# A written order for GpSimd in attention, and a few operations moved in the opening of a transformer layer

## The chip, the cores and the metric

The kernel runs on one core of a Trainium2 chip. Its time is the device time of one execution in microseconds (us). The engines are named as in the profile: PE is TensorE (matrix products), PEld its weight load, DVE is VectorE, ACT is ScalarE, POOL is GpSimd, SP is SyncE, which only issues DMA transfers. Each engine works through its own queue of instructions in the order in which the program lists them.

## The reference

One layer over 1024 latent tokens and 256 context tokens, model width 1024, all in float32. Cut to what matters here:

```
m_lat = silu(c) @ w_mod + b_mod            # six modulation vectors; m_ctx the same from c_ctx
h_lat = rms_norm(x, norm1_g) * (1 + sc1) + sh1
h_ctx = rms_norm(ctx, norm1_g) * (1 + csc1) + csh1
rq, rk, rv, rg, dq, dk, dv = split(h @ w_in)          # rotary positions on q and k
ret = sum over 2 directions of group_norm(retention(rq, rk, rv, decay))    # chunks of 128, states carried
y_ret = silu(rg) * ret
p   = softmax over keys, for two score maps per head  # 4 heads, 1280 keys, queries in blocks of 128
a   = p[0] - lam * p[1]
y_diff = rms_norm(a @ dv) * subln_g * 0.8             # per head, over its 128 columns
x   = x + g1 * (concat(y_ret, y_diff) @ w_out)
h2  = rms_norm(x, norm2_g) * (1 + sc2) + sh2
u   = conv3(h2 @ w_up);  x = x + g2 * ((silu(u_a) * u_b) @ w_down)
out = rms_norm(x, final_g)
```

## The kernel before

**Precision.** A float32 matrix is split in two parts, hi (a cast by ACT) and lo (the difference, by DVE or POOL). A product is three matmuls, hi by hi, hi by lo, lo by hi (`passes`, lines 133 to 135).

**Stages.** The program runs through one core's queues in this order:

- the *opening*: the modulation vectors of the first norm, the norm of the tokens, and the first projection (block 6 of w_in, the values of attention). Per block of 128 model columns `modulate` (lines 585 to 600) transposes four row-scaled token tiles on PE (L590), lets ACT write hi (L593), DVE a float32 copy `tmp` (L598), and DVE or POOL the lo part (L600). `scale` (L584) multiplies a token tile by its row's factor, `power` makes that factor (L115), `mod_part` (L562) makes the modulation and `mod_row` (L566) and `mod_sums` (L573, L574) bring it in place, `w_split` (L621, L623) splits the weights. Token tiles 0 to 3 form half 0, tiles 4 to 7 half 1.
- the other *projections* (blocks 5, 2, 1, 3, 0, 4). Each takes its weights by `split_slice` (lines 193 to 199): load on SP, cast on ACT (L198), difference on DVE (L199).
- *retention*, as side work beside the last projections. `beside(generator, rate, due)` sets a generator, and `tick`, called for each k-step of a projection (three matmuls), adds `rate` to a counter that starts at `due`; for each whole unit of the counter one step of the generator puts out its instructions. Retention's generator is `outputs` (lines 369 to 406), with rate 1.35. Its products of states start at L269; the states are summed on DVE (L466).
- *attention*: 32 units, four heads by eight query tiles. Per unit: scores (L940), their least value (L943, DVE), exp (L947, ACT), the ratio of the two sums (L951 and L952, DVE, 128x1), the combined probabilities (L955, DVE, 128x1280), their transposes (L960 on PE, copies L966 on ACT), values (L972 on PE), copy and square (L976, L981 on ACT), e (L983, POOL, 128x1), the sum for the norm (L986, DVE), the power (L987, POOL, 128x1), the scaling (L990, ACT), a transpose (L994, PE), hi (L998, ACT) and lo (L1001, DVE). The table `TAU` gives each of these a time in units; the operations are written in that order, step n after step n, and `in_order` fixes it for the engines of `FORCE`: PE, DVE, ACT and SP, not for POOL.
- beside attention POOL and ACT prepare the output projection, a Strassen-Winograd product of half matrices. `first_tokens` and `out_weights` load 512 columns into `woraw` (five buffers), ACT casts them (L1123 and L1106), POOL subtracts (L1124, L1108). `joined_tokens` (L1128 to 1132) has POOL add hi and lo of the attention result to a float32 tile, a `woraw` too, and issues DMA transfers that add it to sums in DRAM. Other DMA transfers of POOL (L1156 and around) add weights in DRAM. Queries, keys and values of later units are loaded by POOL's queue (L1018, L1021, L1043). `issue_after` holds such a piece back in the scheduler until a power of an earlier unit has been placed.
- the *output projection* and the *MLP*, which the change does not touch.

The order in the opening is the order of the source from `begin` to `in_order(begin)`; what stands outside (such as the first split of the next block, L198 and L199) is placed by the scheduler.

Of the kernel before, what the change touches and what calls it, by code (L numbers as in the profile page):

```python
# [8 lines left out]
F32 = mybir.dt.float32  # L9
F32R = mybir.dt.float32r  # L10
# [59 lines left out]
def r32(ap):  # L70
    return ap.bitcast(F32)
# [3 lines left out]
def kernel(  # L75
# [85 lines left out]
    with ExitStack() as p1:  # L161
# [385 lines left out]
        with ExitStack() as p0:  # L547
# [151 lines left out]
            for k in range(KD):  # L699
# [8 lines left out]
                if k == 1:  # L708
                    mod_sums(2)
                    latents(0, 2)  # L710
                    for t in (2, 3):
                        scale(xs0[t], 2 + t, 3 * P, D)
                    for q in range(2):
                        mod_part(3, q)
                    mod_row(3)
                if k == 4:
                    square(xs1[2], 8)
                    power(8)
                    scale(xs1[0], 6)
# [15 lines left out]
                if k == 0:  # L735
                    for q in range(2):
                        mod_part(2, q)
                    mod_row(2)
                if 0 < k < KD - 2:
                    mod_sums(k + 2)  # L740
                    latents(0, k + 2)
                    if 0 < k < 5:
                        for q in range(2):
                            mod_part(k + 3, q)
                        mod_row(k + 3)
                if k in (0, 2, 4):
                    w_split()
# [65 lines left out]
        wg = stream_block(5)  # L813
        beside(modulations2(), 37 / 156)
# [96 lines left out]
        beside(outputs(), 1.35, -16.0)  # L911
# [182 lines left out]
    def out_weights(srcs, sl, eng=nc.sync, low=nc.vector, lag=0, after=(), free=0):  # L1094
        raws = []
        srcs = [src[:, k, :] for src in srcs for k in range(4)]
        for k in range(len(srcs) + lag):
            if k < len(srcs):
                raw = wo.tile([P, 512], F32, name="woraw", bufs=5)
                wo_loads.append(eng.dma_start(out=raw, in_=srcs[k]))  # L1100
                raws.append(raw)
            yield
            if k >= lag:
# [3 lines left out]
                part = low.tensor_tensor(out=wlo, in0=raws[k - lag], in1=r32(whi), op=ALU.subtract)  # L1107
# [5 lines left out]
    wo_gen = out_weights((A11, ws_d[0]), wo_first, nc.gpsimd, nc.gpsimd, 2)  # L1113

    def first_tokens():
        raws = []
        for h in range(H + 2):
            if h < H:
                raws.append(wo.tile([P, 512], F32, name="woraw", bufs=5))
                nc.gpsimd.dma_start(out=raws[h], in_=yr_d[:, h, :])  # L1120
            yield
            if h > 1:
                nc.scalar.copy(yT[0][1][:, h - 2, :], raws[h - 2])  # L1123
                nc.gpsimd.tensor_tensor(out=yT[1][1][:, h - 2, :], in0=raws[h - 2], in1=r32(yT[0][1][:, h - 2, :]), op=ALU.subtract)  # L1124

    wo_gen = itertools.chain(first_tokens(), wo_gen)

    def joined_tokens(h, half):  # L1128
        raw = wo.tile([P, 512], F32, name="woraw", bufs=5)
        nc.gpsimd.tensor_tensor(out=raw, in0=r32(yT[0][half][:, H + h, :]), in1=r32(yT[1][half][:, H + h, :]), op=ALU.add)  # L1130
        for to in (t4_d,) if half else (t2_d, t3_d):
            nc.gpsimd.dma_start(out=to[:, h, :], in_=raw, accum_op=ALU.add)

    with ExitStack() as p2:
# [6 lines left out]
        for n in range(n_units + 8):  # L1141
# [3 lines left out]
            if n == 9:  # L1145
                with tc.issue_after(units[n - 5].pool_ins.ins):
                    nc.gpsimd.dma_start(out=g1, in_=row_d[0].rearrange("p c -> (p c)").partition_broadcast(P))
            if n in (6, 9, 15, 17, 21, 28):
                with tc.issue_after(units[n - 5].pool_ins.ins):
                    if n == 6:  # L1150
                        nc.gpsimd.dma_start(out=t1_d[:, H - 1, :], in_=yr_d[:, H - 1, :], accum_op=ALU.add)
                    elif n == 9:
                        nc.gpsimd.dma_start(out=t2_d[:, :, :], in_=t1_d[:, :, :])
                    else:
                        i, j, k = {15: (1, 0, 0), 17: (1, 0, 2), 21: (3, 1, 0), 28: (3, 1, 2)}[n]
                        nc.gpsimd.dma_start(out=ws_d[i][:, k : k + 2, :], in_=ws_d[j][:, k : k + 2, :], accum_op=ALU.add)  # L1156
            if n in (14, 21, 29):
                nc.sync.dma_start(out=t4_d[:, (14, 21, 29).index(n), :], in_=t2_d[:, (14, 21, 29).index(n), :])
            for half, when in ((0, (12, 18, 26, 33)), (1, (16, 24, 31))):
                if n in when:  # L1160
                    with tc.issue_after(units[min(n - 5, n_units - 1)].pool_ins.ins):
                        joined_tokens(when.index(n), half)
            for op, t in order:
# [14 lines left out]
        in_order(start)  # L1178
# [756 lines left out]
```

## Time and profile before

| | us |
|---|---|
| median of 3 runs | 1365.8 (1365.76 to 1365.85) |
| profiled execution | 1365.33, of which span 1363.5 |
| opening | 0 to 65 |
| projections, then with retention beside | 65 to 322, 322 to 460 |
| attention | 460 to 635 |
| output projection, MLP | 635 to 775, 775 to 1363.5 |
| PE busy | 1348.6 of 1363.5 (99%) |
| DVE, ACT, POOL busy | 998.3, 749.6, 341.7 |
| mean granted PE clock of the span | 0.998 |

A row of the timeline reads: start, length, engine, line and operation, output <- inputs, shape and type, how many in a row, and in brackets the idle time of that engine just before and what ended it. The end of a matmul in the profile is modelled, and neighbouring matmuls overlap; so how PE proceeds is read from starts, not from ends. A row with x3 lasts from its first start to its last end.

### The profile page before, as it was taken

How to read it: one execution, taken by the hardware profiler on the slowest of the kernel's cores; microseconds unless marked ns; L12 is line 12 of the kernel's file. 1: busy time of each engine (PE TensorE's matmuls, PEld its weight loads, DVE VectorE, ACT ScalarE, POOL GpSimd, SP SyncE). 2: the span in 40 equal slices, each digit the busy share in tenths (PEclk: the TensorE clock that was granted, in tenths of full speed). 3: DMA queues.
4: the chain of work that ended last, by engine and by line, in shares of the span. 5: the costliest groups of instructions: out<-in, count | busy, mean ns of one | idle time of the engine just before them, and what ended most of it. 6: DMA issues, size and time to landing. Idle time of an engine off the chain costs nothing.

```text
span 1363.5 us, 19850 instructions
## 1 busy us (share of the span) xinstructions
PE 1348.6 (99%) x6978; PEld 1134.9 (83%) x6978; DVE 998.3 (73%) x1514; ACT 749.6 (55%) x1429; POOL 341.7 (25%) x433
## 2 busy tenths in 40 slices
PE   9999999999999999999999999999999999999997
PEld 6788888888898899998887788888888888888886
DVE  4746874425775899897989986677776777798856
ACT  4643312424765789997547555445554455455543
POOL 1210004403776436543021222221222110000001
PEclk9999999999999999999999999999999999999999
DMA  9567897655866769855954898988888875963523
GB/s 369 216 255 241 296 314 245 190 181 157 214 174 168 177 153 182 169 109 157 342 166 113 194 233 217 224 218 226 214 213 214 220 193 172 371 214 101 177 93 124
DMA packets 130492, 279.71 MB, mean 205 GB/s; under 512 B 13700, under 2 KB 34948, under 8 KB 129480
## 3 DMA queue, kind: packets, MB, share of 16 engines
q1 hardware_dynamic: 100440, 212.99, 45.8%
q0 software_dynamic: 29376, 64.00, 25.6%
q10 hardware_dynamic: 576, 1.44, 0.3%
q8 instruction: 55, 0.90, 0.3%
q14 instruction: 45, 0.37, 0.1%
HBM read 212.31 MB, written 69.75 MB: 207 GB/s over the span
## 4 chain that ended last, share of the span: by engine, by line
PE 87%; DVE 5%; ACT 3%; issue 2%; DMA 1%; POOL 1%; POOLq 0%; DVEq 0%; ACTq 0%
PE chain L135 6%; PE chain L133 6%; PE chain L134 6%; PE c L134 5%; PE c L133 5%; PE c L135 5%; PE pv L972 4%; PE pl L133 4%; PE pl L135 4%; PE pl L134 4%; PE pA L940 4%; PE pn L135 3%; PE pn L134 3%; PE pn L133 3%; PE third L134 3%; PE third L133 3%
## 5 line engine op out<-in xcount | busy, mean ns | idle before, releaser
L1269 POOL DMA_DIRECT2D cmb<-w_up x80 | 73.9, 1151 | 180.4 <-DMA cmb<-w_up 142.8
L133 PE MATMUL pl<-hT,whi 128*128 128x512 f32 x256 | 105.4, 412 | 0.0
L133 PE MATMUL chain<-T,whi 128*128 128x512 f32 x264 | 102.9, 391 | 0.0
L134 PE MATMUL chain<-T,whi 128*128 128x512 f32 x264 | 102.6, 389 | 0.0
L135 PE MATMUL chain<-T,wlo 128*128 128x512 f32 x264 | 102.4, 390 | 0.2 <-DVE wlo L1197 0.2
L135 PE MATMUL pl<-hT,wlo 128*128 128x512 f32 x256 | 100.1, 391 | 0.0
L134 PE MATMUL pl<-hT,whi 128*128 128x512 f32 x256 | 99.9, 390 | 0.0
L943 DVE TENSOR_REDUCE mt<-pA 128x1 f32<-128x1280 f32 x64 | 95.2, 1489 | 6.1 <-PE pA L940 4.6
L947 ACT ACTIVATE p<-pA,mt 128x1280 f32<-128x1280 f32 x64 | 85.5, 1336 | 9.4 <-DVE mt L943 8.7
L133 PE MATMUL c<-whi,ghl 128*128 128x512 f32 x232 | 90.2, 389 | 0.0
L134 PE MATMUL c<-wlo,ghl 128*128 128x512 f32 x232 | 90.2, 389 | 0.0
L135 PE MATMUL c<-whi,ghl 128*128 128x512 f32 x232 | 90.2, 389 | 0.0
L940 PE MATMUL pA<-ks,qhl 128*128 128x512 f32 (+1 forms) x384 | 89.6, 368 | 0.6 <-ACT p L947 0.5
L1193 ACT CAST whi<-cmb 128x512 fp32r<-128x512 f32 x60 | 37.5, 627 | 85.2 <-PE chain L134 63.0
L940 PEld LDWEIGHTS pA<-ks,qhl 128*128 128x128 f32 x384 | 68.1, 189 | 12.9 <-ACT p L947 1.3
L972 PE MATMUL pv<-va,aT 128*128 128x128 f32 x640 | 77.3, 276 | 0.8 <-DVE yT L1001 0.5
L972 PEld LDWEIGHTS pv<-va,aT 128*128 128x128 f32 x640 | 74.0, 192 | 2.3 <-DVE yT L1001 1.3
L1193 ACT CAST whi<-wra 128x512 fp32r<-128x512 f32 x54 | 33.1, 623 | 68.9 <-PE third L134 40.2
L133 PE MATMUL third<-yT,whi 128*128 128x512 f32 x168 | 65.4, 389 | 0.0
L134 PE MATMUL third<-yT,whi 128*128 128x512 f32 x168 | 65.4, 389 | 0.0
L135 PE MATMUL third<-yT,wlo 128*128 128x512 f32 x168 | 65.4, 389 | 0.0
L133 PE MATMUL pn<-whi,hT 128*128 128x512 f32 x160 | 64.7, 405 | 0.0
(342 smaller groups left out, 3842.2 us busy)
## 6 DMA issues: line engine op xcount, KB each, us to landing
cmb<-w_up POOLq DMA_DIRECT2D x80, 256.0 KB, 6.5
wm<-w_mod SPq DMA_DIRECT2D x32, 512.0 KB, 5.5
cmb<-w_up SPq DMA_DIRECT2D x60, 256.0 KB, 5.2
raw<-w_in SPq DMA_DIRECT2D x27, 512.0 KB, 5.7
wra<-w_up SPq DMA_DIRECT2D x23, 512.0 KB, 6.2
W<-w_down SPq DMA_DIRECT2D x44, 256.0 KB, 6.2
wrb<-w_up SPq DMA_DIRECT2D x40, 256.0 KB, 4.5
ad<-s SPq DMA_DIRECT2D x20, 512.0 KB, 5.7
```

What stands on the lines that cost most here:

```text
L133: mm(ps, lh, rh, start=first, stop=False, skip_group_check=more)
L134: mm(ps, lh, rl, start=False, stop=False, skip_group_check=more)
L135: return mm(ps, ll, rh, start=False, stop=last, skip_group_check=more)
L940: mm(self.pa[m][:, c0:c1], self.q[:, m, i, qs], self.k[:, m, c0:c1], start=(i == 0), stop=(i == 1))
L943: nc.vector.tensor_reduce(out=self.mt[:, m : m + 1], in_=self.pa[m][:, :LK], axis=AX.X, op=ALU.min)
L947: nc.scalar.activation(self.p[m], self.pa[m][:, :LK], AF.Exp, scale=-1.0, bias=self.mt[:, m : m + 1], accum_out=self.s[:, m : m + 1])
L972: mm(self.pv, self.aT[:, c, :], self.v[:, c, :], start=(c == 0), stop=(c == NKT - 1))
L1193: cast = nc.scalar.copy(hi, src)
L1269: nc.gpsimd.dma_start(out=o, in_=src, accum_op=ALU.add)
```

## The change

Four things are edited.

1. Opening: the scaling of the rest of token tiles 2 and 3 (128x640) moves from k = 1 to the end of k = 0, the scaling of tile 5 (`xs1[1]`) ahead of the modulation of block 6 of half 0; the last weight split is put out in two, its ACT cast earlier.
2. The next projection's first split is bound behind the newest instruction of ACT and of DVE at that place of the opening (L198 and L199).
3. The counter of retention's side work starts at -17.6 in place of -16.0.
4. Attention: `Pool` joins the engines whose order is fixed, and one function, `beside_roots`, puts the side work out right after the power of its step. The subtraction of an item stands one step behind its cast, where it stood in the same step; the joined tiles come from a pool of their own (two buffers); one addition of weights in DRAM moves from step 21 to 22.

The diff, cut where it only takes old lines away:

```diff
@@ opening
                 if k == 1:
                     mod_sums(2)
                     latents(0, 2)
-                    for t in (2, 3):
-                        scale(xs0[t], 2 + t, 3 * P, D)
                     for q in range(2):
                         mod_part(3, q)
                     mod_row(3)
                 if k == 4:
                     square(xs1[2], 8)
+                    w_split(only=nc.scalar)
                     power(8)
                     scale(xs1[0], 6)
...
                         mod_part(2, q)
                     mod_row(2)
+                    for t in (2, 3):
+                        scale(xs0[t], 2 + t, 3 * P, D)
                 if 0 < k < KD - 2:
                     mod_sums(k + 2)
+                    if k == 4:
+                        scale(xs1[1], 7)
                     latents(0, k + 2)
...
-                if k in (0, 2, 4):
+                if k in (0, 2):
                     w_split()
...
                 if k == 4:
                     square(xs1[3], 9)
                     power(9)
-                    scale(xs1[1], 7)
+                    w_split(only=nc.vector)
...
+            newest_of = {ins.engine: ins for ins in nc.cur_bb.bb.instructions[begin:]}
             rtab = load_rope(1)
...
         wg = stream_block(5)
+        order_only(high_parts[0].ins, newest_of[nc.scalar.engine])
+        order_only(low_parts[0].ins, newest_of[nc.vector.engine])
@@ retention
-        beside(outputs(), 1.35, -16.0)
+        beside(outputs(), 1.35, -17.6)
@@ attention
+    def out_ahead():
+        srcs = [yr_d[:, h, :] for h in range(H)] + [w[:, k, :] for w in (A11, ws_d[0]) for k in range(4)]
+        raws, parts = [], []
+        for n in range(len(srcs) + 3):
+            if n > 2:
+                hi, lo = parts[n - 3]
+                nc.gpsimd.tensor_tensor(out=lo, in0=raws[n - 3], in1=r32(hi), op=ALU.subtract)
+            if n < len(srcs):
+                raws.append(wo.tile([P, 512], F32, name="woraw", bufs=5))
+                nc.gpsimd.dma_start(out=raws[n], in_=srcs[n])
+            if 1 < n < len(srcs) + 2:
+                i = n - 2
...
+                cast = nc.scalar.copy(parts[i][0], raws[i])
...
             yield
...
     def joined_tokens(h, half):
-        raw = wo.tile([P, 512], F32, name="woraw", bufs=5)
+        raw = at.tile([P, 512], F32, name="joined", bufs=2)
...
+    def beside_roots(n):
+        for half, when in ((0, (12, 18, 26, 33)), (1, (16, 24, 31))):
+            if n in when:
+                joined_tokens(when.index(n), half)
+                break
+        else:
+            if n >= 9 and n not in (13, 21):
+                next(wo_gen, None)
...
+        elif n in (15, 17, 22, 28):
+            i, j, k = {15: (1, 0, 0), 17: (1, 0, 2), 22: (3, 1, 0), 28: (3, 1, 2)}[n]
+            nc.gpsimd.dma_start(out=ws_d[i][:, k : k + 2, :], in_=ws_d[j][:, k : k + 2, :], accum_op=ALU.add)
...
-                if op == "f" and n >= 9 and n not in (12, 16, 18, 24, 26, 31, 33):
-                    with tc.issue_after(units[min(n - 6, n_units - 1)].pool_ins.ins):
-                        next(wo_gen, None)
+                if op == "f" and u >= 0:
+                    beside_roots(n)
...
-        in_order(start)
+        in_order(start, FORCE + (mybir.EngineType.Pool,))
```

What the engines' queues look like with it, at three places. In the changed file the lines of attention stand 6 to 9 lower: the power is L993, e L989, the subtraction L1125, its load L1128, the joined tile L1145 and its transfers L1147, the addition of weights L1165.

POOL in attention, the stretch that begins at 528.73 us of the trace, before (`ssa` is the sum of the norm, `e` its small term, `woraw` the float32 side tile, `yT` the hi and lo parts, `sgd` and `wsd` sums in DRAM):

```order
L987 TENSOR_TENSOR ssa<-ssa,mhalf 128x1
L1130 TENSOR_TENSOR woraw<-yT_4482,yT_4484 128x512
L983 TENSOR_TENSOR e<-sa 128x1
L1100 DMA woraw<-w_out 128x512
L1132 DMA sgd_155<-woraw 128x512
L1124 TENSOR_TENSOR yT_4484<-woraw,yT_4482 128x512
L987 TENSOR_TENSOR ssa<-ssa,mhalf 128x1
L1156 DMA wsd_157<-wsd_156 128x1024
L983 TENSOR_TENSOR e<-sa 128x1
```

and with the change:

```order
L993 TENSOR_TENSOR ssa<-ssa,mhalf 128x1
L1125 TENSOR_TENSOR yT_4484<-woraw,yT_4482 128x512
L1128 DMA woraw<-w_out 128x512
L1165 DMA wsd_157<-wsd_156 128x1024
L989 TENSOR_TENSOR e<-sa 128x1
L993 TENSOR_TENSOR ssa<-ssa,mhalf 128x1
L1145 TENSOR_TENSOR joined<-yT_4482,yT_4484 128x512
L1147 DMA sgd_155<-joined 128x512
L989 TENSOR_TENSOR e<-sa 128x1
L993 TENSOR_TENSOR ssa<-ssa,mhalf 128x1
```

Between two powers (L987, L993) there were two operations of 128x512 and now there is one, the first thing behind the power.

DVE in the opening, from the modulation of block 6 of half 0 (`hT_186`) to the first of half 1 (`hT_187`), before:

```order
L598 TENSOR_SCALAR tmp<-pt,mcol 128x512
L600 TENSOR_TENSOR hT_186<-tmp,hT_184 128x512
L623 TENSOR_TENSOR wlo<-raw,whi 128x1024
L115 TENSOR_SCALAR sm<-sm 128x1
L584 TENSOR_SCALAR xs_1_214<-xs_1_214,sm 128x1024
L584 TENSOR_SCALAR xs_2_215<-xs_2_215,sm 128x1024
L584 TENSOR_SCALAR xs_3_216<-xs_3_216,sm 128x1024
L573 TENSOR_SCALAR mcol<-pm,bsc,cl 128x2
L574 TENSOR_SCALAR mcol<-pm,cl 128x2
L199 TENSOR_TENSOR wlo<-raw,whi 128x1024
L598 TENSOR_SCALAR tmp<-pt,mcol 128x512 x2
L600 TENSOR_TENSOR hT_187<-tmp,hT_185 128x512
```

and with the change, the same stretch and, behind the mark, the last rows of the modulation of half 1:

```order
L584 TENSOR_SCALAR xs_1_214<-xs_1_214,sm 128x1024
L598 TENSOR_SCALAR tmp<-pt,mcol 128x512
L600 TENSOR_TENSOR hT_186<-tmp,hT_184 128x512
L115 TENSOR_SCALAR sm<-sm 128x1
L623 TENSOR_TENSOR wlo<-raw,whi 128x1024
L584 TENSOR_SCALAR xs_2_215<-xs_2_215,sm 128x1024
L584 TENSOR_SCALAR xs_3_216<-xs_3_216,sm 128x1024
...
L598 TENSOR_SCALAR tmp<-pt,mcol 128x512 x2
L600 TENSOR_TENSOR hT_187<-tmp,hT_185 128x512
L199 TENSOR_TENSOR wlo<-raw,whi 128x1024
L598 TENSOR_SCALAR tmp<-pt,mcol 128x512
L600 TENSOR_TENSOR hT_187<-tmp,hT_185 128x512
```

One scaling has passed the modulation of block 6, and L199 has gone from ahead of half 1's modulations to ahead of their last pair.

PE at the first product of states (`pc`) in the projection that retention runs beside, before and then with the change; each k-step is L133, L134, L135, and a new token half begins with `hT_184`:

```order
L269 MATMUL pc_2970<-st,rk 128x128 x2
L133 MATMUL pl<-hT_185,whi 128x512
L134 MATMUL pl<-hT_187,whi 128x512
L135 MATMUL pl<-hT_185,wlo 128x512
L133 MATMUL pl<-hT_185,whi 128x512
L134 MATMUL pl<-hT_187,whi 128x512
L135 MATMUL pl<-hT_185,wlo 128x512
L133 MATMUL pl<-hT_185,whi 128x512
L134 MATMUL pl<-hT_187,whi 128x512
L135 MATMUL pl<-hT_185,wlo 128x512
L133 MATMUL pl<-hT_184,whi 128x512
```

```order
L269 MATMUL pc_2973<-st,rk 128x128 x2
L133 MATMUL pl<-hT_185,whi 128x512
L134 MATMUL pl<-hT_187,whi 128x512
L135 MATMUL pl<-hT_185,wlo 128x512
L133 MATMUL pl<-hT_185,whi 128x512
L134 MATMUL pl<-hT_187,whi 128x512
L135 MATMUL pl<-hT_185,wlo 128x512
L133 MATMUL pl<-hT_184,whi 128x512
```

The product stands two k-steps ahead of the new half where it stood three: one k-step later.

More of the change, by code (lines that the diff above doesn't have):

```diff
@@ L1092, with out_weights @@
     g1 = wo.tile([P, D], F32, name="g1")
-    def out_weights(srcs, sl, eng=nc.sync, low=nc.vector, lag=0, after=(), free=0):
+    def out_weights(srcs, sl, lag=0, after=(), free=0):
         raws = []
@@ L1099, in out_weights @@
                 raw = wo.tile([P, 512], F32, name="woraw", bufs=5)
-                wo_loads.append(eng.dma_start(out=raw, in_=srcs[k]))
+                wo_loads.append(nc.sync.dma_start(out=raw, in_=srcs[k]))
                 raws.append(raw)
@@ L1106, in out_weights @@
                 wo_casts.append(nc.scalar.copy(whi, raws[k - lag]))
-                part = low.tensor_tensor(out=wlo, in0=raws[k - lag], in1=r32(whi), op=ALU.subtract)
+                part = nc.vector.tensor_tensor(out=wlo, in0=raws[k - lag], in1=r32(whi), op=ALU.subtract)
                 for ins in after if k - lag >= free else ():
@@ L1112 @@
     wo_first, wo_casts, wo_loads = [], [], []
[L1113 to L1118, printed above, removed]
-                raws.append(wo.tile([P, 512], F32, name="woraw", bufs=5))
-                nc.gpsimd.dma_start(out=raws[h], in_=yr_d[:, h, :])
+    def out_ahead():
[6 more added lines that the diff above has]
+            if n < len(srcs):
+                raws.append(wo.tile([P, 512], F32, name="woraw", bufs=5))
+                nc.gpsimd.dma_start(out=raws[n], in_=srcs[n])
+            if 1 < n < len(srcs) + 2:
+                i = n - 2
+                if i < H:
+                    parts.append(tuple(yT[a][1][:, i, :] for a in range(2)))
+                else:
+                    parts.append(tuple(wo.tile([P, 512], F32R, name=nm, bufs=8) for nm in ("wohi", "wolo")))
+                    wo_first.append(parts[i])
+                cast = nc.scalar.copy(parts[i][0], raws[i])
+                if i >= H:
+                    wo_casts.append(cast)
             yield
[L1122 to L1126, printed above, removed]
+    wo_gen = out_ahead()
     def joined_tokens(h, half):
-        raw = wo.tile([P, 512], F32, name="woraw", bufs=5)
+        raw = at.tile([P, 512], F32, name="joined", bufs=2)
         nc.gpsimd.tensor_tensor(out=raw, in0=r32(yT[0][half][:, H + h, :]), in1=r32(yT[1][half][:, H + h, :]), op=ALU.add)
@@ L1132, in joined_tokens @@
             nc.gpsimd.dma_start(out=to[:, h, :], in_=raw, accum_op=ALU.add)
+    def beside_roots(n):
[3 more added lines that the diff above has]
+                break
+        else:
+            if n >= 9 and n not in (13, 21):
+                next(wo_gen, None)
+        if n == 6:
+            nc.gpsimd.dma_start(out=t1_d[:, H - 1, :], in_=yr_d[:, H - 1, :], accum_op=ALU.add)
+        elif n == 8:
+            nc.gpsimd.dma_start(out=g1, in_=row_d[0].rearrange("p c -> (p c)").partition_broadcast(P))
+        elif n == 9:
+            nc.gpsimd.dma_start(out=t2_d[:, :, :], in_=t1_d[:, :, :])
+        elif n in (15, 17, 22, 28):
+            i, j, k = {15: (1, 0, 0), 17: (1, 0, 2), 22: (3, 1, 0), 28: (3, 1, 2)}[n]
+            nc.gpsimd.dma_start(out=ws_d[i][:, k : k + 2, :], in_=ws_d[j][:, k : k + 2, :], accum_op=ALU.add)
     with ExitStack() as p2:
@@ L1144 @@
                 vars(units[n]).update(fore[n])
[L1145 to L1156, printed above, removed]
             if n in (14, 21, 29):
                 nc.sync.dma_start(out=t4_d[:, (14, 21, 29).index(n), :], in_=t2_d[:, (14, 21, 29).index(n), :])
[L1159 to L1162, printed above, removed]
             for op, t in order:
```

## The prediction, on record before the changed kernel ran

> **What bounds the kernel now.** I read the busy times and the chain of waits first. All times are us.
>
> ```profile
> span 1363.5 us, 19850 instructions
> PE 1348.6 (99%) x6978; PEld 1134.9 (83%) x6978; DVE 998.3 (73%) x1514; ACT 749.6 (55%) x1429; POOL 341.7 (25%) x433
> PE 87%; DVE 5%; ACT 3%; issue 2%; DMA 1%; POOL 1%; POOLq 0%; DVEq 0%; ACTq 0%
> ```
>
> TensorE (PE) sets the time nearly everywhere. An edit on GpSimd (POOL), VectorE (DVE) or ScalarE (ACT) can only win what PE loses by waiting for them or by running its work later than it could. Whole-stage shares hide this, because a PE held up inside a stage still counts nearly as busy; attention from its second third on shows how little is left by that measure (columns: window, its length, busy time of PE, weight loads, DVE, ACT, POOL with their instructions, then clock, DMA share, GB/s):
>
> ```profile
> 518.80:635.00 116.20, 115.59 (x846) 105.82 (x844) 103.61 (x139) 105.88 (x247) 61.93 (x89) 1.00 0.70 136
> ```
>
> Only 0.6 idle. So I went by the rhythm instead: attention runs the same unit of work again and again, and the timeline of PE gives the start of each unit's product of probabilities and values.
>
> ```profile
> 466.98 2.40 PE L972 MATMUL pv<-va,aT 128*128 128x128 f32 x20
> ...
> 518.77 2.40 PE L972 MATMUL pv<-va,aT 128*128 128x128 f32 x20
> ...
> 524.72 2.40 PE L972 MATMUL pv<-va,aT 128*128 128x128 f32 x20
> ...
> 530.47 2.40 PE L972 MATMUL pv<-va,aT 128*128 128x128 f32 x20
> ...
> 536.94 2.50 PE L972 MATMUL pv<-va,aT 128*128 128x128 f32 x20 [0.25 <-DVE yT L1001]
> ...
> 631.66 2.39 PE L972 MATMUL pv<-va,aT 128*128 128x128 f32 x20
> ```
>
> From 466.98 to 518.77 lie 9 units: 51.79 / 9 = 5.754 each. From 518.77 to 631.66 lie 19 units in 112.89, where 19 x 5.754 = 109.33 would do. **The later units lose 3.56 together.** Their first three last 5.95, 5.75 and 6.47. What differs from the calm units is the side work, of which POOL and ACT carry the parts of interest here. Who suffers is seen on line 952, a 128x1 operation of DVE on the way to the next probabilities (first the two windows of that line alone, DVE's busy time behind the length; then single rows of DVE and POOL):
>
> ```profile
> 466.00:519.00 53.00, 1.98 (x9) 1.00 0.82 165
> 519.00:632.00 113.00, 8.22 (x19) 1.00 0.70 130
> ```
>
> ```profile
> 528.50 0.16 DVE L986 SCALAR_TENSOR_TENSOR ssa<-e,ssa 128x1 f32<-128x1 f32 x1 [0.54 <-ACT jka L981]
> 528.73 0.56 POOL L987 TENSOR_TENSOR ssa<-ssa,mhalf 128x1 f32<-128x1 f32 x1 [0.73 <-DVE ssa L986]
> 529.28 1.28 POOL L1130 TENSOR_TENSOR woraw<-yT,yT 128x512 f32<-128x512 f32 x1
> 531.91 1.64 POOL L1124 TENSOR_TENSOR yT<-woraw,yT 128x512 fp32r<-128x512 f32 x1
> 531.98 1.59 DVE L952 SCALAR_TENSOR_TENSOR r<-r,sa,nlam 128x1 f32<-128x1 f32 x1 [0.18 <-ACT p L947]
> ```
>
> In calm units line 952 takes 1.98 / 9 = 0.22. At 531.98 it takes 1.59: it starts 0.07 behind a 128x512 subtraction of POOL and ends with it (533.57 against 533.55). This is the unit of 6.47. The 19 later units pay 8.22 - 19 x 0.22 = 4.04 more on that line, not all of it passed on to PE.
>
> A sentence beside it: the Trainium skill (SBUF — State Buffer, Who interferes with whom) says that a VectorE instruction with two inputs in SBUF and a GpSimd instruction that reads SBUF share a pair of ports, and the first keeps it for its whole instruction. By that rule, the trace agrees (1.59 for 0.22).
>
> **The change part by part. Attention, POOL.** A unit's POOL work gets a written order: power (L987), then at most one 128x512 operation, then DMA issues, then e (L983). In the unit above the two 128x512 operations L1130 and L1124 stood behind one power; now no step holds two. The subtraction takes an item whose cast was made a step earlier, so it can start at once. From power to end: L987 starts 0.23 behind L986 (528.73 - 528.50), and ends 0.79 behind it; with the longest operation, 1.64, POOL is done at 0.79 + 1.64 = 2.43. L952 comes 531.98 - 528.50 = 3.48 behind L986. It is free by 1.05, so **all of the 4.04 on L952 should go**. What lies behind is e and the issues:
>
> ```profile
> 507.76 1.83 POOL L1132 DMA_DIRECT2D sgd<-woraw  x2
> 526.48 1.53 POOL L983 TENSOR_TENSOR e<-sa 128x1 f32<-128x1 f32 x1
> ```
>
> After a joined tile with two issues e may start at 0.79 + 1.28 + 1.83 = 3.90, and may last 1.53 if it falls beside the large DVE operation, as at 526.48: end 5.43, against the next L986 at 5.75. Slack 0.32.
>
> The same page's rule speaks against the change here: the blocking goes both ways, so POOL may be held behind the large two-input operation on DVE. By it e ends where I put it; if the hold came on top of a DMA issue, the rival on the strict queue below is what would follow.
>
> **Attention, ACT.** The twelve casts of side tiles stay, one per step, in the same place of ACT's unit:
>
> ```profile
> 518.01 0.62 ACT L1123 CAST yT<-woraw 128x512 fp32r<-128x512 f32 x1
> ```
>
> The first cast lies in the unit of 5.95 (0.20 over calm), the second, one unit on, in one of 5.75 (nothing): ACT is shifted by the first and stays shifted. A run of casts in neighbouring steps thus costs about 0.20 at its first, and again after two, since the lag has gone into the third (my choice). Before there are five runs; now the twelve stand in seven (11; 14, 15; 17; 19, 20; 22, 23; 25; 27 to 29). Charge: 8 x 0.20 = 1.60. **Gain 3.56 - 1.60 = 1.96.** Bounds: 3.56 if the casts hide; 3.56 - 12 x 0.20 = 1.16 if each costs; 0.3 if, further, one collision like 530.47 (0.72) and part of a second remain.
>
> **Retention.** The side work starts 1.6 units of its counter later; at 1.35 per k-step this is 1.2 k-steps, in the order one (three projection matmuls ahead of the first product of states).
>
> ```profile
> 321.42 0.39 PE L135 MATMUL pl<-hT,wlo 128*128 128x512 f32 x1
> 322.22 0.71 PE L269 MATMUL pc<-st,rk 128*128 128x128 f32 x4 [0.41 <-DVE st L466]
> 321.47 0.69 DVE L466 TENSOR_TENSOR st<-st,xb 128x512 f32<-128x512 f32 x1
> ```
>
> Matmuls of this shape follow each other at 0.23, so PE could go on at 321.65; it does at 322.22, after DVE's state sum ends (322.16): 0.57 lost. Three matmuls ahead cover 3 x 0.23 = 0.69. **Gain 0.57**; between 0 (the next product waits instead) and 0.57. The side work ends as much later (1.2 x 3 x 0.23 = 0.8), and attention's first loads stand behind it; I cost that at nothing, taking the projection matmuls around it as its cover; if the scores wait for those loads, it takes the whole gain.
>
> **Opening.** Two row scalings (128x640) go ahead of a weight split, one of 128x1024 ahead of a modulation, and the next projection's first split (L199) far back; one cast (ACT) goes ahead. PE's rows by pairs, each stalled pair beside a quiet one of the same kind:
>
> ```profile
> 26.20 0.42 PE L590 MATMUL pt<-ident,xs 128*128 128x128 f32 x2
> ...
> 27.52 1.07 PE L562 MATMUL pr<-wt,cz 128*32 128x256 f32 x16
> ...
> 31.75 0.64 PE L590 MATMUL pt<-ident,xs 128*128 128x128 f32 x4
> 32.31 1.07 PE L562 MATMUL pr<-wt,cz 128*32 128x256 f32 x16
> ...
> 46.09 0.63 PE L590 MATMUL pt<-ident,xs 128*128 128x128 f32 x4
> 46.48 0.71 PE L637 MATMUL pn<-whi,hT 128*128 128x512 f32 x2
> ...
> 47.96 0.65 PE L590 MATMUL pt<-ident,xs 128*128 128x128 f32 x3
> ...
> 49.19 0.71 PE L637 MATMUL pn<-whi,hT 128*128 128x512 f32 x2
> ...
> 62.36 0.39 PE L134 MATMUL pn<-wlo,hT 128*128 128x512 f32 x1
> 63.02 0.50 PE L135 MATMUL pn<-whi,hT 128*128 128x512 f32 x1 [0.28 <-DVE sm L115]
> ```
>
> Lost: 1.32 - 0.56 = 0.76; 1.23 - 0.39 = 0.84; 0.66 - 0.23 = 0.43: together 2.03. All look removed by the new places, but DVE behind them is full (rows, then its window):
>
> ```profile
> 44.17 0.81 DVE L598 TENSOR_SCALAR tmp<-pt,mcol 128x512 f32<-128x512 f32 x1 [0.91 <-ACT hT L593]
> 46.82 2.23 DVE L584 TENSOR_SCALAR xs<-xs,sm 128x1024 f32<-128x1024 f32 x3
> 49.28 1.22 DVE L199 TENSOR_TENSOR wlo<-raw,whi 128x1024 fp32r<-128x1024 f32 x1
> 50.60:62.97 12.37, 12.07 (x15) 1.00 0.70 267
> ```
>
> The last rows' differences end at 62.97 after 12.07 of work in 12.37. They now hold the 1.22 of L199 as well. The chain starts earlier by 0.76 (PE) and by one scaling, 2.23 / 3 = 0.74, done in the idle 0.91: 1.50, or 1.67 with the rest of that idle. Net 0.28 to 0.45; I take **0.4**, between 0 and 2.03.
>
> **Sum:** 1.96 + 0.57 + 0.4 = 2.93. The profiled execution took 1365.33 (span 1363.5, 1.8 around it), 0.47 under the median of 1365.8; from the median: 1365.8 - 2.93, **1362.9**. After attention I expect no difference over 0.3.
>
> **The rivals.** 0.2% of the median, 2.7, is about what a measurement of this kernel can tell from no change; 1363.1 is that border.
>
> - *As worked out*, 1362.9; own range 1361.9 to 1363.7 (a cast more or less, opening 0 to 1). Chance 0.52.
> - *Casts cost everywhere, opening won nothing*: all twelve at 0.20 leave 1.16 in attention, DVE's chain keeps the opening's end, retention half, 0.2: about 1.4, 1364.4. For it: seven runs instead of five, and DVE at 12.07 of 12.37. Against it: the second cast's unit of 5.75. Chance 0.23. Here belongs also that the change doesn't do what it says: the 1.05 of room is used up by POOL's waits, and L952 goes on being caught; gain near 1.
> - *The opening wins in full*: 2.03 + 0.57 and 2.4 in attention = 5.0, 1360.8. For it: the stalls have their causes moved. Against it: L199 in the chain. Chance 0.15.
> - *Slower: the strict POOL queue.* A DMA issue that waits for a tile now holds everything behind it, powers included. Such a wait is in the trace:
>
> ```profile
> 581.98 0.15 DVE L986 SCALAR_TENSOR_TENSOR ssa<-e,ssa 128x1 f32<-128x1 f32 x1
> 582.60 0.59 POOL L1100 DMA_DIRECT2D woraw<-wsd  x1 [2.15 <-DMA sgd<-woraw]
> 583.21 0.58 POOL L987 TENSOR_TENSOR ssa<-ssa,mhalf 128x1 f32<-128x1 f32 x1
> ```
>
> The power came 1.23 behind L986 for 0.23: 1.00 late. Behind the power wait ACT's norm, PE's transpose, DVE's last rows. With seven joined tiles, five such waits cost 5.0 and leave 5.0 - 2.93 = 2.1: 1367.9; it decides from three on. Against it: the joined tiles get buffers of their own, so a load no longer waits for their writes. Chance 0.10.
>
> **How the numbers follow.** Faster by over 0.2% means under 1363.1: seven tenths of the first case (0.37) and all of the third (0.15): 0.52. Slower takes the last case short of its mildest outcomes: 0.08. Within: 0.40. Range 1360.7 to 1365.7: it holds the first three cases but for their edges.
>
> **What would show it.** Right: line 952 between 519 and 632 near 19 x 0.22 = 4.2; no 128x512 row of POOL across it; eight or fewer units of 5.95 among ones of 5.75; the first product of states directly behind its matmul; the lost 0.76 and 0.84 of the opening gone, and L199 among the last modulations with PE waiting for DVE just ahead of the end of the opening. Wrong: powers over 0.5 behind L986, e held past 5.75, scores waiting for keys at the start of attention, or L952 long again.

## The result, and the profile after

The changed kernel takes 1373.09 us (median of 6 runs, 1371.93 to 1374.12) beside 1365.79 for the kernel before: a ratio of 1.0052 with a 95% interval of 1.0040 to 1.0065. It is **slower by some 7 us**; 1362.9 was forecast, and nothing above 1365.7 was in the range. All times below are us.

The page's totals hide it, as before. First the span and busy times of the changed kernel:

```profile
span 1371.0 us, 19847 instructions
PE 1348.5 (98%) x6978; PEld 1134.2 (83%) x6978; DVE 999.2 (73%) x1514; ACT 748.2 (55%) x1429; POOL 342.6 (25%) x433
```

PE is busy for the same 1348.5 (1348.6 before): the 7.5 more of span is PE waiting. The view of waits (engine, what waited, for whom; us in total, times, longest) says where. PE of the changed kernel from 300 to 470, then from 630 on:

```profile
PE po L277 <- ACT yr L307: 2.2, 1, 2.2
PE pu L349 <- ACT o L282: 1.8, 1, 1.8
PE pt L966 <- DVE xa L462: 1.0, 1, 1.0
PE pA L946 <- DMA ks<-dk: 0.9, 1, 0.9
PE pc L269 <- DVE sc L271: 0.5, 1, 0.5
PE pu L349 <- ACT jk L286: 0.5, 1, 0.5
...
PE o L133 <- DVE gated L1367: 2.9, 2, 2.5
```

The same view of the kernel before, from 300 to 470, has no wait over 0.7 (behind 630 it has none over 0.4):

```profile
PE pt L960 <- DVE xa L462: 0.7, 1, 0.7
PE pA L940 <- ACT p L947: 0.5, 1, 0.5
PE pc L269 <- DVE st L466: 0.4, 1, 0.4
```

So there are three new places: retention (L277, L349, L269); the start of attention, where the scores (L946) wait 0.9 for the keys; and the output projection's first part (L133 behind the gate: the product with g1, `gated`, and its sum with the tokens, `x<-x,gated`). The prediction expected no loss at the first and the last; the second is one of its signs of being wrong, and it had costed it at nothing. The places where it expected gains did gain. Line 952 is line 958 now; its two windows of attention in the changed kernel (DVE's busy time behind the length):

```profile
466.00:519.00 53.00, 1.98 (x9) 1.00 0.63 138
519.00:632.00 113.00, 4.40 (x20) 1.00 0.77 155
```

4.40 / 20 = 0.22 each: no instruction of that line is long any more (8.22 for 19 before).

To add such places up I worked out, for all profiles here, how much each distance between the starts of two neighbouring matmuls exceeds the usual distance of that pair of forms (its first quartile), and summed it by stretch. It is a calculation from the records, not a view. In most rows the sum moves as the span does, to within 0.4; in two, attention alone and the later start with pinned loads, it grows by 3.9 and 4.7 where the span grows by 2.2 and 3.3, because the usual distances, taken in each profile by itself, come out shorter there. With those of the kernel before, these two sums are 44.9 and 46.0, and attention alone has 5.6 in 65-345 and 7.5 in 476-635.

| PE's lost time in | 0-65 | 65-345 | 345-445 | 445-476 | 476-635 | 635-680 | 680-end | sum | median | ratio (95%) |
|---|---|---|---|---|---|---|---|---|---|---|
| before | 12.5 | 5.7 | 4.9 | 3.2 | 9.0 | 1.2 | 6.3 | 42.8 | 1365.8 | |
| changed | 10.8 | 5.7 | 11.1 | 4.2 | 7.2 | 5.0 | 6.2 | 50.2 | 1373.1 | 1.0052 (1.0040-1.0065) |
| later start alone | 12.5 | 4.9 | 10.3 | 3.1 | 9.1 | 2.0 | 6.3 | 48.3 | 1372.8 | 1.0047 (1.0034-1.0059) |
| opening alone | 11.3 | 6.0 | 4.9 | 3.2 | 9.3 | 1.4 | 6.3 | 42.3 | 1364.2 | 0.9986 (0.9977-0.9995) |
| attention alone | 12.9 | 6.7 | 5.3 | 3.2 | 7.8 | 4.3 | 6.5 | 46.7 | 1367.9 | 1.0015 (1.0006-1.0024) |
| later start, loads pinned | 12.6 | 6.2 | 7.3 | 4.3 | 9.3 | 1.5 | 6.3 | 47.5 | 1368.6 | 1.0021 (1.0012-1.0030) |
| attention, sums later | 12.6 | 6.2 | 5.1 | 3.1 | 7.7 | 5.7 | 6.4 | 46.8 | 1369.1 | 1.0023 (1.0014-1.0032) |
| ... and joined early | 12.4 | 5.7 | 4.9 | 3.2 | 8.5 | 2.0 | 6.4 | 43.0 | 1365.9 | 0.9999 (0.9990-1.0007) |
| attention, e early | 12.6 | 5.8 | 4.9 | 3.2 | 8.2 | 5.8 | 6.2 | 46.6 | 1368.9 | 1.0022 (1.0012-1.0032) |
| attention, both early | 12.4 | 6.1 | 4.9 | 3.2 | 8.4 | 1.1 | 6.3 | 42.4 | 1364.3 | 0.9989 (0.9980-0.9997) |
| opening + attention, both early | 11.2 | 5.6 | 4.8 | 3.3 | 7.7 | 0.9 | 6.1 | 39.7 | **1363.1** | 0.9981 (0.9972-0.9990) |
| all of the change, mended | 10.7 | 5.5 | 6.7 | 3.2 | 7.6 | 0.9 | 6.3 | 40.9 | 1364.9 | 0.9990 (0.9981-0.9999) |

The changed kernel wins 1.7 in the opening and 1.8 in attention, and loses 6.2 in retention, 1.0 at the start of attention and 3.8 behind attention: 7.4 in all, against 7.5 of span.

### The profile page after: what moved, and what is told of

Read it like the earlier page. It is cut to its first block, busy times and chain, and to the rows that moved or that the text cites. A ratio compares the mean times of both kernels' runs of the same rounds, so it can differ in the third digit from the quotient of the medians.

```text
span 1371.0 us, 19847 instructions
## 1 busy us (share of the span) xinstructions
PE 1348.5 (98%) x6978; PEld 1134.2 (83%) x6978; DVE 999.2 (73%) x1514; ACT 748.2 (55%) x1429; POOL 342.6 (25%) x433
## 4 chain that ended last, share of the span: by engine, by line
PE 84%; DVE 6%; DMA 4%; ACT 3%; issue 2%; POOL 2%; SPq 0%; POOLq 0%; DVEq 0%; ACTq 0%
PE chain L135 6%; PE chain L133 6%; PE chain L134 6%; PE pA L946 5%; PE c L134 5%; PE c L133 5%; PE c L135 5%; PE pv L978 5%; PE pn L135 3%; PE pn L134 3%; PE pn L133 3%; PE pl L133 3%; PE pl L135 3%; PE pl L134 3%; PE third L135 3%; PE third L133 3%
## 5 line engine op out<-in xcount | busy, mean ns | idle before, releaser
L133 PE MATMUL pl<-hT,whi 128*128 128x512 f32 x256 | 105.4, 412 | 0.0
L133 PE MATMUL chain<-T,whi 128*128 128x512 f32 x264 | 102.9, 391 | 0.0
L134 PE MATMUL chain<-T,whi 128*128 128x512 f32 x264 | 102.6, 389 | 0.0
L135 PE MATMUL chain<-T,wlo 128*128 128x512 f32 x264 | 102.3, 390 | 0.2 <-DVE wlo L1213 0.2
L135 PE MATMUL pl<-hT,wlo 128*128 128x512 f32 x256 | 100.1, 391 | 0.0
L134 PE MATMUL pl<-hT,whi 128*128 128x512 f32 x256 | 99.9, 390 | 0.0
L946 PE MATMUL pA<-ks,qhl 128*128 128x512 f32 (+1 forms) x384 | 89.6, 369 | 1.4 <-DMA ks<-dk 0.9
L133 PE MATMUL c<-whi,ghl 128*128 128x512 f32 x232 | 90.2, 389 | 0.0
L134 PE MATMUL c<-wlo,ghl 128*128 128x512 f32 x232 | 90.2, 389 | 0.0
L135 PE MATMUL c<-whi,ghl 128*128 128x512 f32 x232 | 90.2, 389 | 0.0
L946 PEld LDWEIGHTS pA<-ks,qhl 128*128 128x128 f32 x384 | 67.9, 189 | 13.9 <-DVE mt L949 1.3
L1209 ACT CAST whi<-wra 128x512 fp32r<-128x512 f32 x54 | 33.1, 623 | 72.4 <-PE third L134 42.3
L135 PE MATMUL third<-yT,wlo 128*128 128x512 f32 x168 | 65.4, 389 | 0.0
L134 PE MATMUL third<-yT,whi 128*128 128x512 f32 x168 | 65.4, 389 | 0.0
L133 PE MATMUL third<-yT,whi 128*128 128x512 f32 x168 | 65.4, 389 | 0.0
L133 PE MATMUL pn<-whi,hT 128*128 128x512 f32 x160 | 64.8, 405 | 0.0
```

The costliest lines, as they stand in the source:

```text
L133: mm(ps, lh, rh, start=first, stop=False, skip_group_check=more)
L134: mm(ps, lh, rl, start=False, stop=False, skip_group_check=more)
L135: return mm(ps, ll, rh, start=False, stop=last, skip_group_check=more)
L946: mm(self.pa[m][:, c0:c1], self.q[:, m, i, qs], self.k[:, m, c0:c1], start=(i == 0), stop=(i == 1))
L1209: cast = nc.scalar.copy(hi, src)
```

## The experiments

### The three parts alone

The edits sort themselves by stage: each part alone reorders the queues in its own stage and nowhere else (attention's also in the first part of the output projection). First the later start of retention:

```diff
-        beside(outputs(), 1.35, -16.0)
+        beside(outputs(), 1.35, -17.6)
```

> The kernel before with the later start of retention's side work alone (-17.6 for -16.0). Theory A (the later start reorders the loads on SP; three loads of the states' inputs stand behind a load that waits for a buffer): PE stalls of about 2.0, 0.6, 2.3 and 0.7 in retention as in the changed kernel, 1.0 more at the start of attention, 0.6 won at the first product of states: 1365.8 + 5.6 + 1.0 - 0.6, about 1371.8. Rival (the stalls come from the weight loads that the opening's edit moves, or from transfers that differ from run to run): about 1365.2.

Measured: 1372.76 (1370.88 to 1373.36) beside 1366.02, 1.0047. Theory A's size holds (1371.8 expected). Of its places in retention, three are in this run's profile (by the calculation 2.3 at L277 near 399, and 0.7 twice). The stall of 2.0 at L349 near 371 is not; in its place PE loses 1.1 near 355, at a product of states that waits for DVE. The 1.0 at the start of attention is not there either (3.1 for 3.2 before), so that loss of the changed kernel is not the later start's alone.

Then the opening's edits and the first split of the next block, and nothing else of the diff:

> The kernel before with the edits of the opening and the first split of the next block alone. If the changed kernel's opening is the opening's own: PE wins 1.7 up to 65 us and loses 0.7 at 222: about 1364.8. My prediction's step: 0.4 won, 1365.4. If what is won there is given back by the weights of the next projection, 1365.8.

Measured: 1364.17 (1363.61 to 1365.50), 0.9986 with 0.9977 to 0.9995: 1.85 won, more than four times my step's 0.4. Two rows of PE in each kernel show why: the matmul that waits for the last modulated block, and the first transpose of the context rows behind it. Before, then the opening alone:

```profile
63.02 0.50 PE L135 MATMUL pn<-whi,hT 128*128 128x512 f32 x1 [0.28 <-DVE sm L115]
...
65.66 0.27 PE L590 MATMUL pt<-ident,xc 128*128 128x128 f32 x1
```

```profile
62.88 0.50 PE L135 MATMUL pn<-whi,hT 128*128 128x512 f32 x1 [0.22 <-DVE hT L600]
...
64.61 0.27 PE L590 MATMUL pt<-ident,xc 128*128 128x128 f32 x1
```

DVE's chain does end where L199 lets it, 0.14 earlier (62.88 for 63.02). But in the new order PE has more matmuls ahead of the one that waits and fewer behind it: ten lie between it and the context's transpose before, six now. PE used the time that it won, 5 x 0.23 = 1.15 of it (four fewer behind, and the transpose stands one matmul further back), and 0.14 + 1.15 = 1.29; the table has 1.2. The rest of the 1.85 is not located: the span of this profile is only 0.5 shorter than that of the kernel before.

The attention part alone:

> The kernel before with the new POOL order in attention alone. Theory: 1.8 won within attention (my step said 1.96), 3.5 lost behind it in the output projection, where the second load of a sum stands on SP ahead of the token loads and waits for the last joined tile: about 1367.5. Rival (that loss comes from the shift in time that the earlier stages hand on, not from this edit): about 1364.0.

Measured: 1367.90 (1365.34 to 1369.71), 1.0015 with 1.0006 to 1.0024. Both halves of the theory are there: 1.2 won between 476 and 635 (1.5 by the usual distances of the kernel before), and 3.1 lost from 635 to 680, without the other edits. By the medians against the kernel before, the parts give +6.7 - 1.85 + 1.9 = +6.8, and the whole +7.3: they add.

### Retention: the order of loads on SP

What PE waits for in the changed kernel is ACT, and what ACT waits for is a load. SP's rows, ACT's and PE's, in the order of time:

```profile
364.49 0.32 SPq L242 DMA_DIRECT2D kvo<-kvg  x1
364.90 0.38 SPq L242 DMA_DIRECT2D kvs<-kvg  x1
...
368.15 0.51 ACT L333 ACTIVATE ks<-kvs,kd 128x256 f32<-128x256 f32 x1 [5.74 <-DMA kvs<-kvg]
...
369.30 0.38 ACT L307 ACTIVATE yr<-pyt 128x256 f32<-128x256 f32 x1
...
370.32 0.59 ACT L282 COPY o<-po 128x512 f32<-128x512 f32 x1
370.96 0.49 PE L349 MATMUL pu<-kvs,ks 128*128 128x128 f32 x2 [1.83 <-ACT o L282]
```

The load kvs (keys and values for a sum of states) is issued 0.41 behind the load kvo (keys and values for an output), which was issued only when a buffer came free. ACT sits 5.74 at the scaling L333, and L282, for which PE waits, stands behind it. In the kernel before the same two loads stood the other way round, and kvs was out 4.2 earlier than kvo:

```profile
360.22 0.32 SPq L242 DMA_DIRECT2D kvs<-kvg  x1
364.43 0.32 SPq L242 DMA_DIRECT2D kvo<-kvg  x1
```

In the run with the later start alone the two loads go out in the same order and as late, kvs at 365.14. There PE itself, behind the 1.1 that it lost near 355, comes to L349 so late that it hardly waits:

```profile
371.22 0.49 PE L349 MATMUL pu<-kvs,ks 128*128 128x128 f32 x2
```

To tell the loads' order from ACT's and POOL's new order, three loads were put back, with the start at -17.6:

```diff
...
+            for o, s in ((8, 25), (10, 30), (12, 34)):
+                if (nm, n_kv[nm]) in (("kvo", o), ("kvs", s)) and ("kvo", o) in kv_loads and ("kvs", s) in kv_loads:
+                    order_only(kv_loads["kvo", o].ins, kv_loads["kvs", s].ins)
```

> The later start of retention alone, with three loads on SP (kvo, numbers 8, 10, 12) put back behind the kvs load that stood ahead of them in the kernel before; ACT, DVE, POOL and PE keep the order of the later start. Theory A (SP's order makes the stalls): the stalls at L349 and L277 vanish, 1365.2 to 1366.2. Rival (ACT's new order, or the later start itself, makes them): as the later start alone, about 1371 to 1372.

Measured: 1368.56 (1367.12 to 1371.81), 1.0021. The waits at L349 and L277 are gone, with ACT, DVE, POOL and PE in the order of the later start; by the medians 4.2 of the 6.7 come back (3.0 in the table's third column). Theory A holds for these, and the rest falls between both forecasts: 2.5 stays. In this run's waits of PE, from 340 to 480, two products of states and the first transposes of attention come first:

```profile
PE pt L966 <- DVE xa L468: 1.4, 1, 1.4
PE pc L275 <- DMA rk<-rk: 1.2, 1, 1.2
PE pc L275 <- DVE sc L277: 0.6, 1, 0.6
```

Is it the load order whichever way the start moves, or lateness? Two other starts (-15.0 and -16.8) change SP's order at one place each:

> The kernel before with retention's side work started earlier instead of later (-15.0 for -16.0). On SP the load kvo 8 now stands ahead of kvs 25, as with -17.6, while kvo 10 and kvo 12 stand behind kvs 30 and kvs 34 as in the kernel before. Theory A (the place of kvo ahead of kvs makes the stall): PE waits about 2 at L349 near 370 and does not wait at L277 near 398; 1 to 3 slower. Rival (lateness of the side work makes it): no stall, as fast as before or faster.

Measured: 1367.84 (1366.21 to 1369.58), 1.0015 with 1.0006 to 1.0024. An earlier start is slower too, so lateness as such is not it. But theory A's place was wrong: no wait at L349 near 370. kvo 8 went out at 361.77 (364.49 in the changed kernel) and kvs 25 at 362.18, early enough. PE waited elsewhere:

```profile
PE pc L269 <- DMA rk<-rk: 2.0, 1, 2.0
PE pyt L301 <- POOL y L296: 0.9, 1, 0.9
```

> The kernel before with -16.8, half the change's shift. On SP only kvo 12 stands ahead of its kvs (34); kvo 8 and 10 stand as before. Theory A: PE waits about 2.3 at L277 near 398 and does not wait at L349 near 370; 1.5 to 3 slower. Rival (lateness): half of all the stalls of -17.6, at both places.

Measured: 1368.39 (1366.90 to 1370.47), 1.0017 with 1.0008 to 1.0027. The size fits theory A, the place only in part: 0.9 at L277 near 403 (waiting for DVE by the view, not for ACT), nothing at 370, and 0.6 or 0.7 at two more places. **What holds:** with -17.6 the stalls at L349 and L277, the two largest of the changed kernel, go when three loads on SP no longer stand behind a load without a buffer; the whole change, mended below, doesn't have them either (0.9 and 0.8 at two products of states are its largest in this stage). **What doesn't:** that the order of the two decides by itself; it does when the buffer is late. All three other starts cost 1.9 to 6.7, each at places of its own.

### Behind attention: the last joined tile and the last e on POOL

In the changed kernel SP stands for 12 in the second load of the sums, and the token loads (`x<-x`) follow it; DVE's gate waits for the tokens, and PE for what stands behind the gate:

```profile
633.59 12.54 SPq L1351 DMA_DIRECT2D raw<-sgd  x2
646.23 1.41 SPq L1244 DMA_DIRECT2D x<-x  x3
...
654.56 0.69 DVE L1368 TENSOR_TENSOR x<-x,gated 128x512 f32<-128x512 f32 x1 [6.13 <-DMA x<-x]
...
668.42 0.47 PE L133 MATMUL o<-wohi,yT 128*128 128x512 f32 x1 [2.48 <-DVE gated L1367]
```

The token loads came at 636.19 in the kernel before. Theory B takes the place of that load on SP as the cause. The loads of the second and third sum were put behind token loads:

```diff
...
+        if src is t2_d or src is t3_d:
+            order_only(got.ins, x1_loads[6 if src is t2_d else 3].ins)
```

> The attention edit alone, with the second and third load of the sums (raw<-sgd) on SP put behind the token loads x_6 and x_3. Theory B (SP waits 12 us in the second of these loads for the last joined tile, and the token loads behind it come late): the stalls of 2.4 and 0.6 at L133 near 663 vanish, 1366.0 - 1.8, about 1364.3. Rival (the last joined tile itself is late, since POOL now holds it behind a power, and PE waits for the sum made from it): PE waits elsewhere in the output projection and the time stays near 1367.9.

Measured: 1369.10 (1367.76 to 1371.33), 1.0023: **theory B fell.** The waits near 663 are gone and one of 3.0 has come near 647, at the last transpose of attention. SP was not held by the sum, and the token loads were still issued only at 640.09. POOL, SP and DVE of this run:

```profile
634.36 0.55 POOL L987 TENSOR_TENSOR ssa<-ssa,mhalf 128x1 f32<-128x1 f32 x1 [4.86 <-DVE ssa L986]
634.88 1.28 POOL L1139 TENSOR_TENSOR joined<-yT,yT 128x512 f32<-128x512 f32 x1
637.06 1.79 POOL L1141 DMA_DIRECT2D sgd<-joined  x2 [0.90 <-POOL joined L1139]
...
639.35 0.56 POOL L987 TENSOR_TENSOR ssa<-ssa,mhalf 128x1 f32<-128x1 f32 x1 [0.27 <-DVE ssa L986]
639.88 0.18 POOL L983 TENSOR_TENSOR e<-sa 128x1 f32<-128x1 f32 x1
640.09 1.37 SPq L1238 DMA_DIRECT2D x<-x  x3
...
645.79 0.69 DVE L1364 TENSOR_TENSOR x<-x,gated 128x512 f32<-128x512 f32 x1 [5.38 <-DMA x<-x]
```

The token loads go out 0.03 behind the end of the last e (639.88 + 0.18 = 640.06). e is 128x1; it reads the sums `sa` of the last unit, and is the last to read them. The strict order holds it behind the power of the unit before the last, and the last joined tile behind a power that waits 4.86 for DVE. In the kernel before, POOL took both while it waited:

```profile
631.45 1.28 POOL L1130 TENSOR_TENSOR woraw<-yT,yT 128x512 f32<-128x512 f32 x1 [1.16 <-DVE r L951]
...
635.15 0.86 POOL L987 TENSOR_TENSOR ssa<-ssa,mhalf 128x1 f32<-128x1 f32 x1
635.68 0.48 POOL L983 TENSOR_TENSOR e<-sa 128x1 f32<-128x1 f32 x1
...
640.05 0.55 POOL L987 TENSOR_TENSOR ssa<-ssa,mhalf 128x1 f32<-128x1 f32 x1 [3.88 <-DVE ssa L986]
```

Here e ends at 636.16 and the token loads go out at 636.19. Next, the joined tile was put ahead of its step's power, with the sums still later:

```diff
+            if n == 33:
+                beside_roots(n)
             for op, t in order:
...
-                if op == "f" and u >= 0:
+                if op == "f" and u >= 0 and n != 33:
```

> As the run with the sums' loads put later, and with the last joined tile on POOL ahead of its step's power instead of behind it (it then starts some 4 us earlier). Theory B: the tile's lateness costs nothing once SP isn't held by it: 1364.3 again. Rival: 0.5 to 3 faster than the run without this.

Measured: 1365.92 (1365.03 to 1366.64), 0.9999: 3.2 faster than the run without it, as the rival said. Yet the last e hasn't moved, and the token loads are issued at 640.04, as before the move (640.09). Only POOL's order differs between the two runs. What moved is the loads' arrival, which the gate's row shows:

```profile
640.04 1.28 SPq L1240 DMA_DIRECT2D x<-x  x3
...
643.68 0.69 DVE L1366 TENSOR_TENSOR x<-x,gated 128x512 f32<-128x512 f32 x1 [3.24 <-DMA x<-x]
```

The gate goes on 3.6 behind the issue, where it took 5.7 with the joined tile's transfers issued from 637.06 on, shortly ahead of the token loads (632.89 here). Behind this row stand on DVE the last sum for the norm, and with it the last power, ACT's scaling and PE's last transpose, whose wait falls from 3.0 to 0.8. With the opening's edits added to each of the two:

> The edits of the opening and of attention, retention as before, and the sums' loads later. If the parts add: 1366.0 - 1.8 (opening, measured alone) - 1.7 = 1362.5. If the stages share one slack: 1364.

Measured: 1369.09 (1365.49 to 1371.80), 1.0019 with 1.0011 to 1.0027. The 1362.5 was theory B's and fell with it; the wait at the last transpose is 2.2 here.

> As the run with opening and attention, and the last joined tile ahead of its power: 1362.5 by theory B, up to 3 less by the rival.

Measured: 1363.91 (1363.29 to 1365.47), 0.9985 with 0.9976 to 0.9994. The two parts' gains add now.

Theory C names e. In the next kernel only e moved: that of the last unit (`small` writes e) is put out right behind that of the unit before it, the joined tile and SP left alone:

```diff
...
+                if self is units.get(n_units - 2):
+                    units[n_units - 1].small()
...
```

> The attention edit alone, with one POOL operation moved: e of the last unit (128x1) directly behind e of the unit before, so that it no longer stands behind that unit's power. Theory C (the token loads x_4 to x_6 wait for this e, the last reader of the memory that they take; the strict order put it 4 us later, DVE's gate waits for the tokens, and PE for what stands behind the gate): x_4 is issued 4 to 5 us earlier than in the runs with the attention edit, the stalls of 2.4 to 3.0 vanish, 1366.0 - 1.8, about 1364.3. Rival (the last joined tile is what comes late): 1367 to 1368.

Measured: 1368.88 (1366.76 to 1371.06), 1.0022: not what theory C expected, and nearer to the rival, the late joined tile. The rows say why: e now stands behind the joined tile's transfers, and these behind the power that waits.

```profile
634.33 0.55 POOL L993 TENSOR_TENSOR ssa<-ssa,mhalf 128x1 f32<-128x1 f32 x1 [4.87 <-DVE ssa L992]
634.85 1.27 POOL L1145 TENSOR_TENSOR joined<-yT,yT 128x512 f32<-128x512 f32 x1
637.02 1.79 POOL L1147 DMA_DIRECT2D sgd<-joined  x2 [0.90 <-POOL joined L1145]
638.20 0.98 POOL L989 TENSOR_TENSOR e<-sa 128x1 f32<-128x1 f32 x2
639.21 1.30 SPq L1244 DMA_DIRECT2D x<-x  x3
...
645.87 0.69 DVE L1368 TENSOR_TENSOR x<-x,gated 128x512 f32<-128x512 f32 x1 [5.50 <-DMA x<-x]
```

e ends at 639.18 and the loads go out at 639.21: one us won of four. At the gate nothing is won: its row starts at 645.87, for 645.79 with the late e. Both moved, then, and the sums later as well (SP has the token loads ahead of the second load of the sums in both of these runs):

> As the run before this one, and also the last joined tile ahead of its power and the sums' loads later. Theory C: nothing more to win, 1364.3. Rival: 1364.3 where the run with e alone gave 1367 to 1368.

Measured: 1364.25 (1363.52 to 1365.03), 0.9989 with 0.9980 to 0.9997; 1.1 lost from 635 to 680, as before the change (1.2). POOL and SP:

```profile
630.87 1.27 POOL L1145 TENSOR_TENSOR joined<-yT,yT 128x512 f32<-128x512 f32 x1 [1.20 <-DVE r L951]
...
635.11 0.62 POOL L989 TENSOR_TENSOR e<-sa 128x1 f32<-128x1 f32 x2
635.75 1.35 SPq L1246 DMA_DIRECT2D x<-x  x3
```

In all of these kernels where SP is not held by a sum, the token loads follow the end of the last e by 0.02 to 0.03 (636.16, 640.06, 640.01, 639.18, 635.73). The chain from POOL's order through e to the issue of the token loads, and from their arrival through DVE's gate to PE, is shown. Between issue and arrival stands the joined tile a second time. By the medians, with the sums later: 1369.10 with both late, 1365.92 with the joined tile early, 1364.25 with both early; with e alone early 1368.88. The joined tile is worth 3.2 by itself, e 0.2 by itself and 1.7 behind the joined tile. So e is the smaller part, and the joined tile matters not only because e stands behind it: its transfers, out shortly ahead of the token loads, go with a later arrival. How they hold the loads up no run shows.

> The changed kernel with retention's start as before (-16.0) and the last e early. Parts add: 1366.0 - 1.8 (opening) - 1.8 (attention) = 1362.4.

Measured: 1366.81 (1364.91 to 1371.12), 1.0009 with 1.0000 to 1.0017; missed, and with the joined tile late as in the run with e alone.

> As the run before this one, with the last joined tile ahead of its power and the sums' loads later: 1362.4 by theory C; less, if the joined tile still holds something.

Measured: **1363.05** (1361.58 to 1364.83), 0.9981 with 0.9972 to 0.9990: the best version, 2.85 faster than the kernel before and 10 faster than the change as it stood.

### Everything of the change, mended

The whole change with its later start, the three loads pinned, joined tile and e early, sums later:

> The whole changed kernel, with its later start of retention, and with all three mendings: the three loads pinned on SP, the last joined tile and the last e early on POOL, the sums' loads later. If these causes and the rest of the shift (2.5 slower when pinned) are all there is: 1363.05 + 2.5 = 1365.6. If a cause is missing: above 1367.

Measured: 1364.90 (1362.42 to 1366.22), 0.9990 with 0.9981 to 0.9999. The causes account for the loss of the changed kernel: it goes from 1.0052 to 0.9990 without giving up any of the edits. What the later start still costs is 6.7 for 4.8 in the table's third column.

## Why the prediction was wrong, step by step

- **Attention, POOL: right.** L952 fell to 0.22 each; no 128x512 row of POOL lies across it. **Attention, ACT: right.** The units with a cast that opens a run, and the third of the run of three, take 5.92 to 5.95 in the changed kernel, eight as charged; of the four second ones two take 5.77, the others 5.97 and 5.85. From start to start of the values the changed kernel loses 1.92 over the 21 units from 512.88 to 635.63, where 1.60 was forecast; the kernel before lost 3.56 over the same units: a gain of 1.64 for 1.96.
- **Retention: the 0.57 was won and the price was missed.** The first product of states follows its matmul at once, as the two rows of PE show:

```profile
320.97 0.39 PE L135 MATMUL pl<-hT,wlo 128*128 128x512 f32 x1
321.20 0.70 PE L269 MATMUL pc<-st,rk 128*128 128x128 f32 x4
```

The step "in the order one (three projection matmuls ahead of the first product of states)" costed a new start by PE's row alone. The scheduler gave SP, ACT and POOL a new order for the whole stage; the runs put 6.7 on it, 4.2 of them on three loads. The part "attention's first loads stand behind it; I cost that at nothing" held in the run with the later start alone. In the changed kernel the scores do wait for them, 0.9 for the keys (`ks<-dk` in the view above), which POOL issued at 438.08 (432.29 before); that is the case that the prediction named and gave no cost. The later start alone issues them at 438.35 and doesn't wait, so what makes the difference is open, and so is the 1.1 that the run with pinned loads lost there.
- **Opening: right in sign, mis-sized.** The term 0.4 measured 1.85 (0.7 to 3.1). The two stalls went as forecast: in the changed kernel 0.56 stands for 1.32 at the first pair of rows, 0.54 for 1.23 at the second. DVE's end moved by 0.14 in the run with the opening alone and by 0.70 in the changed kernel (62.27 for 62.97), around the 0.28 to 0.45 that I gave it; the step that failed is that PE's time ends with DVE's chain. PE had five more matmuls ahead of its wait, and the wait itself stayed.
- **"After attention I expect no difference over 0.3": wrong, 3.8.** This is the second failed step. The new order of SP behind attention was there to be read before the run, and I took it for harmless; but as the fallen theory B shows, SP's order alone was not the cause; POOL's was: with the sums out of the way the joined tile still stood 3.4 later than in the kernel before (634.88 for 631.45) and e 3.9 later.
- **The rival "the strict POOL queue"** had the right mechanism, that what POOL waits for holds all behind it, with the wrong instruction waiting. I priced a power that stands behind a waiting DMA issue. What happened is the reverse: a joined tile and an e stand behind a power that waits 4.9 for DVE. No DMA issue on POOL made a power late: in the changed kernel each of attention's powers starts 0.24 to 0.25 behind its L992. The place was the last step, where work behind the power has no next unit to hide in.
- By the sum: forecast -2.93; measured -1.85 (opening), -1.7 (attention's own gain), +6.7 (start), +3.6 (the end of attention: +1.9 + 1.7), together +6.8. Together the gains were larger than forecast; two losses that had no term decided.

## What to carry to other kernels

Where an edit is costed, compare the order of every queue in its stage, the one that only issues transfers included, and follow each moved load to who waits for it; an edit of a start time or of a fixed order is an edit of all of them. When an engine's order is fixed, look at the last step by itself: a tiny instruction there can be the last reader of memory that the next stage's loads need, and a late transfer can go with a late arrival of the loads issued behind it. And try the parts alone first: here two were good, one was bad, and one good one hid a loss of its own that two small moves took away.

## What the runs showed that was not expected

- Kernels in which PE waits for a chain of transfers also spread more. The 33 runs of the kernel before in one comparison lay within 1364.92 to 1367.24; beside them opening and attention with the sums later ran from 1365.49 to 1371.80, and with the joined tile early from 1363.29 to 1365.47.
- In four profiles with attention's edit (joined early alone, e early with and without the opening, both early) PE waits once near 536 for keys of a new head (`ks<-dk`): 1.0, 1.9, 0.7 and 0.7; in the others not. It is not tied to one of the edits by these profiles, since both early with the opening has none; its cause was not tried.
- A start moved by 0.8, 1.0 or 1.6 of the side work's counter cost 2.5, 1.9 and 6.7: not in order of its size.
